# A hybrid decoder step on one core: gate and value rows change banks, token statistics are summed first, and the last convolution adds nothing by DMA

## The chip, the cores and the metric

The kernel runs on one core of a Trainium2 chip. Five engines work side by side, each with its own queue in program order: TensorE (PE in the profile; PEld is its weight load), VectorE (DVE), ScalarE (ACT), GpSimd (POOL) and SyncE (SP). SP starts the ordinary transfers, GpSimd the transfers that add into their destination. The metric is the device time of one execution in microseconds; lower is better.

## The reference

One layer of a decoder for 1024 prompt tokens and 8 sample tokens (1032 columns), width 1024, all in float32. Cut to what matters:

```python
h = rmsnorm(x, norm_g)
a_val, a_gl, a_gate, b_u, b_v, b_gate = split(h @ w_in)       # six groups of 1024 columns
a_in  = a_val * sigmoid(a_gl)
a_conv = depthwise_conv(concat([conv_buf, a_in]), conv_w) + conv_b      # 31 taps
a_out = silu(layernorm(a_conv, a_ln_g, a_ln_b)) * silu(a_gate)
gated = spatial_gate(layernorm(b_v, b_ln_g, b_ln_b), w_s, b_s)          # per head, chunks of 128
b_out = b_u * gated * silu(b_gate)
y = rmsnorm(x + concat([a_out, b_out]) @ w_out, final_g)
```

The last 30 rows of `a_in` (prompt and samples) and rows of `b_v` are outputs too.

## The kernel before, in words

**Layout.** Channels lie on the 128 partitions, tokens along the free axis. `w_in` has 48 column tiles of 128 channels: values 0 to 7, sigmoid gates 8 to 15, gates of a 16 to 23, `b_u` 24 to 31, `b_v` 32 to 39, gates of b 40 to 47.

**Units.** A unit makes two column tiles, its row 0 and its row 1 (`mts`, L124): P (value and sigmoid gate of the convolution), v (two tiles of `b_v`), B (`b_u` and its gate, one head), G (two gates of a). There are 24, in the order of L122. The first two, P0 and P1, are worked on together, first for the first half of the tokens and then for the second; each of the others takes all tokens, as two halves (lanes) of 516 columns.

**Seven products for eight.** The two column tiles, the two halves of the 1024 inputs and the two quarters of a lane's tokens form a 2x2 block product, done in Strassen and Winograd's way with seven products (`PRODS`, L36) in place of eight. VectorE makes the sums of weights (`wsum`) and of inputs (`xform`) for it. Float32 precision comes from splitting each operand in two parts, H (ScalarE's rounded copy) and L (VectorE's remainder): H·H + H·L + L·H.

**Slots.** A unit runs in seven slots, a product each, of 24 matmuls over 258 columns. Products gather in PSUM banks: slot 0 writes bank a, slot 1 bank e; then ScalarE copies a to b and e to a tile `p7`; slot 2 adds into b, which ScalarE copies to c; slot 3 adds into a, slot 4 into b, slot 5 into c, slot 6 into b. So a is full after slot 3 (half of row 0), b after slot 4 (half of row 1, still lacking `p7`), c after slot 5 (the other half of row 1, lacking `p7`), and b after slot 6 (the other half of row 0). The next unit's slot 0 writes bank a again.

**Taking the rows out of the banks.** `evac1` (L283): VectorE adds `p7` to bank b or c into row 1; for all but v ScalarE then applies sigmoid or SiLU in place. `evac0` (L272): for v and G ScalarE takes row 0 out of the bank, after slot 3 (L889) and in the next unit's slot 0 (L866). For P and B VectorE multiplies bank a or b by row 1 (L277), in the middle of slot 6 (L870) and in the next unit's slot 0. `finish` (L567) then starts what follows: the convolution for P, a product with the spatial gate `t2` for B.

**Convolution.** `conv_items` (L315) puts a tile's 31 taps on a list. Tap 0 and 1 are ScalarE's (L323, L325), 21 taps are VectorE's, alternately into `c` and `accb` (L333); for the last GT = 8 taps ScalarE makes a product (`gtap`, L341), with every second VectorE tap, and GpSimd adds these by DMA into two of them (L345). `fin` adds `accb` to `c` on VectorE (L356) and the two products by DMA (L358). `acc_item` then adds `c` to the channel sum `ssum` by DMA and stores it (L311, L312).

**LayerNorm behind it.** `mean` (L372) multiplies `ssum` by ones on TensorE. `cen` loads each tile back, subtracts the mean, ScalarE squares, `qacc` sums the squares (L392, L403). `var`, `ln_bc`, then per tile a normalisation and a gate (L456, L462).

**The planner.** `pump` (L99) runs in the middle and at the end of each slot and takes list items while VectorE's planned time is less than 1 us ahead of TensorE's; the program's own prices count, such as MMT = 0.118 a matmul, 1.2 a tap and 1.15 a full row. TensorE items of the list run from slot 3 on; a bar holds `ln_bc` and what follows until all units are done.

**Token statistics.** For each half of the tokens, `stat_x` (L170) squares four x tiles on ScalarE; 48 matmuls of one column sum them over channels; `rstd_x` (L181) takes the root on GpSimd in three pieces; `bcast_x` (L187) spreads it over partitions; `scale_x` (L196) scales x. The first half's come ahead of all products, the second half's in TensorE's queue ahead of slot 0 of the first unit (L833).

**Output.** `w_out` is applied in three groups of columns, each with 8 tiles from b's rows (half 1) and then 8 from a's (half 0), 24 matmuls each (`mmo`, L635); weights are split in two parts as before (L607, L609). Half 0 of group 0 needs the whole LayerNorm.

Of the kernel before, what the change touches and what calls it, by code (L numbers as in the profile page):

```python
# [15 lines left out]
NP_ = 1024  # L16
# [12 lines left out]
GT = 8  # L29
NU = 51  # L30
MMT = 0.118
# [9 lines left out]
def body(ctx, tc, xT, w_in, w_out, state, stateT, conv_w, vecs, wsT, w00, b_s,  # L41
# [80 lines left out]
    units = [(n[0], int(n[1])) for n in ("P0 P1 v0 v1 P2 v2 v3 P3 G0 B0 P4 B1 B2 P5 B3 P6 B4 B5 P7 B6 B7 G1 G2 G3"  # L122
                                         ).split()]
    mts = {"P": lambda k: (k, 8 + k), "v": lambda j: (32 + 2 * j, 33 + 2 * j), "B": lambda h: (24 + h, 40 + h),  # L124
# [43 lines left out]
    CH = tuple((128 * i, n) for i, n in enumerate((128, 128, 2)))  # L168

    def stat_x(p, q, ps):  # L170
        sq = U([128, 2, 2, PW], f"xsq{p}_{q}")
        A.activation(sq, X[p, q], AF.Square)
        for t in range(2):
            for a in range(2):
                for i, (o, n) in enumerate(CH):
                    c = 3 * a + i
                    T.matmul(ps[:n, 0, c:c + 1], lhsT=sq[:, t, a, o:o + n], rhs=ones_m[:, :1],
                             start=(q == 0 and t == 0 and c == 0), stop=(q == 3 and t == 1),
                             skip_group_check=True)

    def rstd_x(p, ps):  # L181
        for (n, a) in ((128, 0), (128, 1), (2, 2)):
            V.tensor_scalar(out=xrs[:n, p, a:a + 4:3], in0=ps[:n, 0, a:a + 4:3], scalar1=EPS, scalar2=None, op0=ALU.add)
            G.tensor_tensor(out=xrs[:n, p, 6 + a:6 + a + 4:3], in0=xrs[:n, p, a:a + 4:3], in1=nhalf[:n, :2],
                            op=ALU.pow)

    def bcast_x(p, ps):  # L187
        for a in range(2):
            for i, (o, n) in enumerate(CH):
                c = 6 + 3 * a + i  # L190
                T.matmul(ps[:, a, o:o + n], lhsT=xrs[:n, p, c:c + 1].to_broadcast([n, 128]), rhs=ident[:n, :n],
                         start=True, stop=True)
        xr[p] = U([128, 2, PW], f"xr{p}")
        A.activation(xr[p], ps[:, :, :PW], AF.Copy)

# [66 lines left out]
    def rows(lanes, r):  # L262
        for u, p in lanes:
            if (u, r) not in row:
                kind, k = units[u]
                if r == 0 and kind == "P":
                    row[u, r] = (U([128, H + NT], f"apad{k}"), H)
                else:
                    row[u, r] = (U([128, NT], f"row{r}_{u}"), 0)
        return {u: row[u, r] for u, p in lanes}  # L270

    def evac0(lanes, z, lohi):  # L272
        kind = units[lanes[0][0]][0]
        if kind in "PB":
            r1 = rows(lanes, 1)
            for (sl, src, dst), (_, _, g) in zip(spots(lanes, rows(lanes, 0), z, lohi), spots(lanes, r1, z, lohi)):
                V.scalar_tensor_tensor(out=dst, in0=src, scalar=-1.0, in1=g, op0=ALU.mult, op1=ALU.mult)  # L277
            dve(0.66)
            return
        for sl, src, dst in spots(lanes, rows(lanes, 0), z, lohi):  # L280
            A.activation(dst, src, FUNC[kind], scale=-1.0)

    def evac1(lanes, z, p7, lohi):  # L283
        kind = units[lanes[0][0]][0]
        for sl, src, dst in spots(lanes, rows(lanes, 1), z, lohi):
            V.tensor_tensor(out=dst, in0=src, in1=p7[:, sl, :], op=ALU.add)
            if kind != "v":
                A.activation(dst, dst, FUNC[kind])
# [13 lines left out]
    cc = {}  # L302

    def acc_item(k):
        def acc():
            c = cc.pop(k)
            if k == 0:
# [5 lines left out]
        fill.append(("dve", 0.0, acc))  # L313

    def conv_items(k, ap):  # L315
        st = {}

# [19 lines left out]
        def gtap(j):  # L337

            def f():
                p = U([128, NP_], f"prod{k}_{j}")  # L340
                A.activation(p, ap[:, j:j + NP_], AF.Copy, scale=cw[:, k, j:j + 1])  # L341
                if j < CW - GT + 2:
# [4 lines left out]
        for j in range(2, CW - GT):  # L347
            fill.append(("dve", 1.2, tap(j)))
            if j % 2 == 0 and j // 2 <= GT:
                fill.append(("dve", 0.0, gtap(CW - GT + j // 2 - 1)))  # L350
            if j == 8 and k:
                acc_item(k - 1)

        def fin():
            c = st["c"]
            V.tensor_tensor(out=c[:, :NP_], in0=c[:, :NP_], in1=st["b"], op=ALU.add)  # L356
            for e in range(2):
                G.dma_start(c[:, :NP_], st.pop(("g", e)), accum_op=ALU.add)  # L358
# [4 lines left out]
    lnc = {}  # L363

    def ln_items():
# [21 lines left out]
        def cen(k):  # L387
            def f():
                c = lnc[k]
                if k < 6:  # L390
# [176 lines left out]
    def finish(u):  # L567
# [3 lines left out]
        if kind == "P":  # L571
            V.memset(r0[:, :H], 0.0)
# [480 lines left out]
```

## Time and profile before

| | us |
|---|---|
| two timed runs | 984.47 and 985.22, median 984.85 |
| the profiled execution | 987.2 |
| its span on the core | 985.3 |
| TensorE busy | 807.6 (82%) |
| VectorE busy | 650.8 (66%) |
| ScalarE busy | 414.1 (42%) |
| GpSimd busy | 82.4 (8%) |
| mean granted TensorE clock | 0.914 |

A row of stretches gives, after its bounds and length, the busy time (and instructions) of PE, PEld, DVE, ACT and POOL, the granted TensorE clock, the share of the DMA engines and GB/s. A group's row gives the source line, the engine, the operation, output<-inputs, shapes and count, then the busy time and the mean duration in ns, then the idle time of that engine just before these instructions and who ended it. A row of the timeline gives start and duration in us, engine, line, operation, and in brackets the idle time before it and who ended it. One matmul of the statistics counts as two records (two passes); those of the products count as one.

### The profile page before, as it was taken

How to read it: one execution, taken by the hardware profiler on the slowest of the kernel's cores; microseconds unless marked ns; L12 is line 12 of the kernel's file. 1: busy time of each engine (PE TensorE's matmuls, PEld its weight loads, DVE VectorE, ACT ScalarE, POOL GpSimd, SP SyncE). 2: the span in 40 equal slices, each digit the busy share in tenths (PEclk: the TensorE clock that was granted, in tenths of full speed). 3: DMA queues.
4: the chain of work that ended last, by engine and by line, in shares of the span. 5: the costliest groups of instructions: out<-in, count | busy, mean ns of one | idle time of the engine just before them, and what ended most of it. 6: DMA issues, size and time to landing. Idle time of an engine off the chain costs nothing. (4 is left out here: it accounts for less than half of the span.)

```text
span 985.3 us, 14147 instructions
## 1 busy us (share of the span) xinstructions
PE 807.6 (82%) x5712; PEld 785.5 (80%) x5712; DVE 650.8 (66%) x805; ACT 414.1 (42%) x562; POOL 82.4 (8%) x103
## 2 busy tenths in 40 slices
PE   7487779979959888998887987999286539999995
PEld 7387779979959888988887887999275528998995
DVE  0527778878875976886767777779245485654754
ACT  2314344545535365354364365346043253513431
POOL 0110001102011111002011101002100000000000
PEclk9997889989979999998989989999688579999998
DMA  7004025658455657458437547449848982284371
GB/s 264 0 1 154 12 66 128 156 135 193 122 140 139 177 136 175 111 132 172 134 94 172 131 115 170 121 109 224 265 145 298 359 327 87 85 286 164 86 258 45
DMA packets 67081, 149.94 MB, mean 152 GB/s; under 512 B 7400, under 2 KB 28584, under 8 KB 67000
## 3 DMA queue, kind: packets, MB, share of 16 engines
q1 hardware_dynamic: 55496, 107.02, 31.9%
q0 software_dynamic: 11520, 42.01, 21.5%
q8 instruction: 45, 0.74, 0.3%
q14 instruction: 20, 0.16, 0.0%
HBM read 84.11 MB, written 28.07 MB: 114 GB/s over the span
## 5 line engine op out<-in xcount | busy, mean ns | idle before, releaser
L244 PE MATMUL za<-hnB,H 128*128 128x258 f32 x384 | 91.4, 325 | 70.7 <-DVE apad L277 41.4
L641 PE MATMUL po<-mh,wh 128*128 128x384 f32 (+1 forms) x384 | 126.2, 329 | 24.2 <-ACT wh L607 16.9
L244 PEld LDWEIGHTS za<-hnB,H 128*128 128x128 f32 x384 | 71.8, 229 | 73.7 <-ACT vh L534 30.5
L641 PE MATMUL po<-mh,wl 128*128 128x384 f32 (+1 forms) x384 | 124.6, 324 | 0.7 <-DVE wl L609 0.7
L641 PE MATMUL po<-ml,wh 128*128 128x384 f32 (+1 forms) x384 | 124.3, 324 | 0.3 <-DVE ml L632 0.3
L155 DVE TENSOR_TENSOR L<-R,H 128x1024 fp32r<-128x1024 f32 x72 | 87.8, 1220 | 48.7 <-ACT H L154 48.3
L333 DVE SCALAR_TENSOR_TENSOR c<-apad,cw,c 128x1024 f32<-128x1024 f32 x88 | 112.4, 1278 | 9.0 <-ACT c L323 9.0
L333 DVE SCALAR_TENSOR_TENSOR accb<-apad,cw,accb 128x1024 f32<-128x1024 f32 x80 | 102.2, 1277 | 0.0
L641 PEld LDWEIGHTS po<-mh,wh 128*128 128x128 f32 x384 | 73.4, 191 | 28.0 <-ACT wh L607 17.2
L154 ACT ACTIVATE H<-R 128x1024 fp32r<-128x1024 f32 x72 | 74.4, 1048 | 37.2 <-DVE R L142 35.9
L244 PE MATMUL za<-hnB,L 128*128 128x258 f32 x384 | 89.1, 319 | 0.0
L244 PE MATMUL za<-lnB,H 128*128 128x258 f32 x384 | 89.0, 318 | 0.0
L244 PE MATMUL zb<-hT,H 128*128 128x258 f32 x384 | 80.9, 292 | 4.4 <-ACT H L154 3.9
L244 PE MATMUL zb<-hT,L 128*128 128x258 f32 x384 | 78.9, 286 | 0.8 <-DVE L L155 0.7
L244 PE MATMUL zb<-lT,H 128*128 128x258 f32 x384 | 78.6, 287 | 0.7 <-DVE lT L230 0.7
L609 DVE TENSOR_TENSOR wl<-wr,wh 128x1024 fp32r<-128x1024 f32 x48 | 58.5, 1223 | 30.1 <-ACT wh L607 28.6
L641 PEld LDWEIGHTS po<-mh,wl 128*128 128x128 f32 x384 | 73.2, 191 | 2.0 <-DVE wl L609 2.0
L641 PEld LDWEIGHTS po<-ml,wh 128*128 128x128 f32 x384 | 73.4, 191 | 0.6 <-DVE ml L632 0.6
L341 ACT ACTIVATE prod<-apad,cw 128x1024 f32<-128x1024 f32 x64 | 73.1, 1143 | 1.5 <-DMA prod<-prod 0.9
L345 POOL DMA_DIRECT2D prod<-prod x48 | 41.2, 859 | 376.0 <-ACT prod L341 316.2
L244 PEld LDWEIGHTS za<-hnB,L 128*128 128x128 f32 x384 | 71.7, 228 | 0.0
L244 PEld LDWEIGHTS za<-lnB,H 128*128 128x128 f32 x384 | 71.3, 226 | 0.0
(149 smaller groups left out, 1632.1 us busy)
## 6 DMA issues: line engine op xcount, KB each, us to landing
R<-w_in SPq DMA_DIRECT2D x96, 256.0 KB, 3.5
prod<-prod POOLq DMA_DIRECT2D x48, 512.0 KB, 5.0
wr<-w_out SPq DMA_DIRECT2D x48, 512.0 KB, 4.6
c<-prod POOLq DMA_DIRECT2D x16, 512.0 KB, 4.6
x<-xT SPq DMA_DIRECT2D x8, 516.0 KB, 8.0
ssum<-c POOLq DMA_DIRECT2D x8, 516.0 KB, 7.0
cD<-c POOLq DMA_DIRECT2D x8, 516.0 KB, 8.2
sgD<-row SPq DMA_DIRECT2D x8, 516.0 KB, 4.8
```

The lines of the kernel that those rows point to most:

```text
L154: A.activation(h, r, AF.Copy)
L155: V.tensor_tensor(out=l, in0=r, in1=h, op=ALU.subtract)
L244: T.matmul(z[:, s, :PW], lhsT=HL[u, wi][we][:, wh, cs], rhs=F[name, p][xe][:, kt, :], start=first, stop=(kt == 3 and we == 1), skip_group_ ...
L333: V.scalar_tensor_tensor(out=o, in0=ap[:, j:j + NP_], scalar=cw[:, k, j:j + 1], in1=o, op0=ALU.mult, op1=ALU.add)
L341: A.activation(p, ap[:, j:j + NP_], AF.Copy, scale=cw[:, k, j:j + 1])
L345: G.dma_start(st["g", j % 2], p, accum_op=ALU.add)
L609: V.tensor_tensor(out=wl[s], in0=r, in1=wh[s], op=ALU.subtract)
L641: T.matmul(z, lhsT=w[:, cs], rhs=m_[g, half, kt][e], start=(half == 1 and kt == 0 and e == 0 and w is wh[s]), stop=(half == 0 and kt == KT ...
```

## The change

- P and B swap their rows: row 0 is now the gate, row 1 the value. ScalarE applies sigmoid or SiLU with a sign change straight from bank a after slot 3 and from bank b in the next unit's slot 0, as for v and G; VectorE's sums with `p7` give the value; in `finish` one multiplication over 1032 columns joins them, on VectorE. Only G keeps an in-place SiLU on row 1.
- Ten taps go to ScalarE and the adding DMAs for tiles 0 to 6, one with each of VectorE's first ten taps, and none for tile 7, whose 29 other taps are VectorE's. Tile 7 is added to the channel sum by VectorE and stays on the chip.
- P7 moves ahead of B5, MMT becomes 0.12.
- x is loaded ahead of the weights. The squares of four x tiles are summed on VectorE, then 12 matmuls of one column (six token groups of 86, two halves) sum over channels; the root is taken in one piece. 16 and 24 matmuls without a use (`warm`) stand before the first half's statistics and behind its broadcast. The second half's statistics go into the slots of the first unit: squares after slot 1, sums after slot 2, matmuls after slot 3, broadcast after slot 4.

```diff
-GT = 8
+GTS = (10,) * 7 + (0,)
-MMT = 0.118
+MMT = 0.12
...
-    units = [... "P0 P1 v0 v1 P2 v2 v3 P3 G0 B0 P4 B1 B2 P5 B3 P6 B4 B5 P7 B6 B7 G1 G2 G3" ...]
-    mts = {"P": lambda k: (k, 8 + k), ..., "B": lambda h: (24 + h, 40 + h),
+    units = [... "P0 P1 v0 v1 P2 v2 v3 P3 G0 B0 P4 B1 B2 P5 B3 P6 B4 P7 B5 B6 B7 G1 G2 G3" ...]
+    mts = {"P": lambda k: (8 + k, k), ..., "B": lambda h: (40 + h, 24 + h),
...
+    CN = PW // 3
+    def square_x(p, q):
         sq = U([128, 2, 2, PW], f"xsq{p}_{q}")
         A.activation(sq, X[p, q], AF.Square)
+        xsq[p, q] = sq
+    def sum_x(p):
+        for q in range(1, 4):
+            V.tensor_tensor(out=xsq[p, 0], in0=xsq[p, 0], in1=xsq.pop((p, q)), op=ALU.add)
+        dve(3.5)
+    def stat_x(p, ps):
+        sq = xsq.pop((p, 0))
+        for c in range(6):
+            for t in range(2):
+                T.matmul(ps[:CN, 0, c:c + 1], lhsT=sq[:, t, c // 3, CN * (c % 3):CN * (c % 3) + CN], rhs=ones_m[:, :1],
+                         start=t == 0, stop=t == 1)
     def rstd_x(p, ps):
+        V.tensor_scalar(out=xrs[:CN, p, :6], in0=ps[:CN, 0, :6], scalar1=EPS, scalar2=None, op0=ALU.add)
+        G.tensor_tensor(out=xrs[:CN, p, 6:], in0=xrs[:CN, p, :6], in1=nhalf[:CN, :6], op=ALU.pow)
...
+    def warm(n):
+        p = PS("e", f"warm{slotno[0]}_{n}")
+        for _ in range(n):
+            T.matmul(p[:, 0, :128], lhsT=ones_m, rhs=ident, start=True, stop=True)
...
     def evac0(lanes, z, lohi):
-        kind = units[lanes[0][0]][0]
-        if kind in "PB":
-            r1 = rows(lanes, 1)
-            for (sl, src, dst), (_, _, g) in zip(spots(lanes, rows(lanes, 0), z, lohi), spots(lanes, r1, z, lohi)):
-                V.scalar_tensor_tensor(out=dst, in0=src, scalar=-1.0, in1=g, op0=ALU.mult, op1=ALU.mult)
-            dve(0.66)
-            return
         for sl, src, dst in spots(lanes, rows(lanes, 0), z, lohi):
-            A.activation(dst, src, FUNC[kind], scale=-1.0)
+            A.activation(dst, src, FUNC[units[lanes[0][0]][0]], scale=-1.0)
     def evac1(lanes, z, p7, lohi):
...
-            if kind != "v":
-                A.activation(dst, dst, FUNC[kind])
+            if units[lanes[0][0]][0] == "G":
+                A.activation(dst, dst, AF.Silu)
...
         def acc():
             c = cc.pop(k)
+            if k == 7:
+                V.tensor_tensor(out=Ssum[0], in0=Ssum[0], in1=c, op=ALU.add)
+                lnc[7] = c
+                return
...
-        for j in range(2, CW - GT):
+        for j in range(2, CW - gt):
             fill.append(("dve", 1.2, tap(j)))
-            if j % 2 == 0 and j // 2 <= GT:
-                fill.append(("dve", 0.0, gtap(CW - GT + j // 2 - 1)))
-            if j == 8 and k:
+            if j < 2 + gt:
+                fill.append(("dve", 0.0, gtap(CW - gt + j - 2)))
+            if j == 10 and k:
                 acc_item(k - 1)
...
-            for e in range(2):
-                G.dma_start(c[:, :NP_], st.pop(("g", e)), accum_op=ALU.add)
+            if gt:
+                for e in range(2):
+                    G.dma_start(c[:, :NP_], st.pop(("g", e)), accum_op=ALU.add)
...
         if kind == "P":
-            V.memset(r0[:, :H], 0.0)
+            V.memset(r1[:, :H], 0.0)
+            V.tensor_tensor(out=r1[:, H:], in0=r1[:, H:], in1=r0, op=ALU.mult)
+            dve(1.25)
...
         if kind == "B":
-            V.tensor_tensor(out=r0, in0=r0, in1=t2.pop(k), op=ALU.mult)
-            dve(1.15)
+            V.tensor_tensor(out=r1, in0=r1, in1=t2.pop(k), op=ALU.mult)
+            V.tensor_tensor(out=r1, in0=r1, in1=r0, op=ALU.mult)
+            dve(2.3)
...
-                if slot == 6 and kind in "PB":
-                    evac0(lanes, Z.pop("a"), 0)
...
-                elif slot == 3 and kind not in "PB":
+                elif slot == 3:
                     evac0(lanes, Z.pop("a"), 0)
```

The start, with the places where the second half's statistics go:

```diff
+        for q in range(4):
+            load_x(0, q)
         for u in range(2):
             wload(u, 1)
...
-        for q in range(4):
-            stat_x(0, q, p)
+        for q in range(4):
+            square_x(0, q)
+        sum_x(0)
+        warm(16)
+        p = PS("e", "xst0")
+        stat_x(0, p)
         rstd_x(0, p)
         for u in range(2):
             wsum(u, "S3")
+            wsum(u, "S1")
             wsplit(u, 1)
-            wsum(u, "S1")
         bcast_x(0, PS("e", "xbc0"))
-        p1 = PS("a", "xst1")
+        warm(24)
...
                 if slot == 1:
                     xform(0, "nB21")
+                    for q in range(4):
+                        square_x(1, q)
                 if slot == 2:
...
+                    sum_x(1)
                 if slot == 3:
...
+                    p = PS("e", "xst1")
+                    stat_x(1, p)
+                    rstd_x(1, p)
                 if slot == 4:
+                    bcast_x(1, PS("e", "xbc1"))
```

More of the change, by code (lines that the diff above doesn't have):

```diff
@@ L119, in slot_end @@
             outq.popleft()[1]()
-    units = [(n[0], int(n[1])) for n in ("P0 P1 v0 v1 P2 v2 v3 P3 G0 B0 P4 B1 B2 P5 B3 P6 B4 B5 P7 B6 B7 G1 G2 G3"
+    units = [(n[0], int(n[1])) for n in ("P0 P1 v0 v1 P2 v2 v3 P3 G0 B0 P4 B1 B2 P5 B3 P6 B4 P7 B5 B6 B7 G1 G2 G3"
                                          ).split()]
-    mts = {"P": lambda k: (k, 8 + k), "v": lambda j: (32 + 2 * j, 33 + 2 * j), "B": lambda h: (24 + h, 40 + h),
+    mts = {"P": lambda k: (8 + k, k), "v": lambda j: (32 + 2 * j, 33 + 2 * j), "B": lambda h: (40 + h, 24 + h),
            "G": lambda q: (16 + 2 * q, 17 + 2 * q)}
@@ L166, in load_x @@
                      xT[256 * q:256 * q + 256, 2 * PW * p:2 * PW * (p + 1)].rearrange("(t p) s -> p t s", p=128))
-    CH = tuple((128 * i, n) for i, n in enumerate((128, 128, 2)))
-    def stat_x(p, q, ps):
+    CN = PW // 3
+    xsq = {}
+    def square_x(p, q):
         sq = U([128, 2, 2, PW], f"xsq{p}_{q}")
         A.activation(sq, X[p, q], AF.Square)
[L173 to L179, printed above, removed]
+        xsq[p, q] = sq
@@ L181, in rstd_x @@
+    def sum_x(p):
[8 more added lines that the diff above has]
+                         start=t == 0, stop=t == 1)
     def rstd_x(p, ps):
[L182 to L185, printed above, removed]
+        V.tensor_scalar(out=xrs[:CN, p, :6], in0=ps[:CN, 0, :6], scalar1=EPS, scalar2=None, op0=ALU.add)
+        G.tensor_tensor(out=xrs[:CN, p, 6:], in0=xrs[:CN, p, :6], in1=nhalf[:CN, :6], op=ALU.pow)
@@ L187, in bcast_x @@
     def bcast_x(p, ps):
[L188 to L192, printed above, removed]
+        for c in range(6):
+            T.matmul(ps[:, c // 3, CN * (c % 3):CN * (c % 3) + CN], lhsT=xrs[:CN, p, 6 + c:7 + c].to_broadcast([CN, 128]),
+                     rhs=ident[:CN, :CN], start=True, stop=True)
@@ L265, in rows @@
                 kind, k = units[u]
-                if r == 0 and kind == "P":
+                if r == 1 and kind == "P":
                     row[u, r] = (U([128, H + NT], f"apad{k}"), H)
@@ L302, in body @@
     cc = {}
+    lnc = {}
     def acc_item(k):
@@ L312, in acc @@
             G.dma_start(cD[k], c)
-        fill.append(("dve", 0.0, acc))
+        fill.append(("dve", 1.15 if k == 7 else 0.0, acc))
     def conv_items(k, ap):
         st = {}
+        gt = GTS[k]
         def start():
@@ L341, in f @@
                 A.activation(p, ap[:, j:j + NP_], AF.Copy, scale=cw[:, k, j:j + 1])
-                if j < CW - GT + 2:
+                if j < CW - gt + 2:
                     st["g", j % 2] = p
@@ L389, in f @@
                 c = lnc[k]
-                if k < 6:
+                if k < 5:
                     lnload(k + 2)
@@ L742, in body @@
     with tc.manual_schedule():
+        for q in range(4):
+            load_x(0, q)
         for u in range(2):
             wload(u, 1)
-        for q in range(2):
-            load_x(0, q)
         SP.dma_start(vec, vecs)
-        for q in range(2, 4):
-            load_x(0, q)
-        for u in range(2):
-            wload(u, 4)
-        for u in range(2):
-            wload(u, 3)
+        for i in (4, 3, 2):
+            for u in range(2):
+                wload(u, i)
         for q in range(4):
             load_x(1, q)
-        for u in range(2):
-            wload(u, 2)
         SP.dma_start(cw, conv_w)
@@ L832, in body @@
                 if slot in (0, 1):
-                    if si == 0 and slot == 0:
-                        for q in range(4):
-                            stat_x(1, q, p1)
-                        rstd_x(1, p1)
                     Z[bank] = PS(bank, f"z{bank}{si}")
```

10 lines of the change are left out of this document (3 added, 7 removed).

## The prediction, made before the changed kernel ran

> **What bounds the kernel now.** I read the span in stretches first, then the groups by line with what ended the idle time before them, then the timeline around the longest waits.
>
> ```profile
> span 985.3 us, 14147 instructions
> core 0: us, PE busy (x) PEld busy (x) DVE busy (x) ACT busy (x) POOL busy (x), PEclk, DMA share, GB/s
> 60.98:135.80 74.82, 54.06 (x348) 50.82 (x349) 51.81 (x75) 28.79 (x42) 4.33 (x4) 0.87 0.20 65
> 135.80:696.44 560.64, 497.81 (x3856) 491.59 (x3856) 434.33 (x515) 272.55 (x374) 64.99 (x78) 0.93 0.59 145
> 662.88:683.32 20.44, 20.44 (x171) 20.23 (x169) 19.32 (x21) 12.28 (x17) 5.51 (x7) 1.00 0.90 221
> 584.21:614.65 30.44, 25.41 (x186) 25.07 (x187) 21.22 (x25) 16.11 (x24) 4.88 (x6) 0.89 0.65 152
> 728.90:810.24 81.34, 44.36 (x230) 42.22 (x228) 49.90 (x51) 32.82 (x38) 2.19 (x2) 0.76 0.85 318
> 810.24:985.30 175.06, 158.56 (x1002) 154.25 (x1002) 94.93 (x136) 60.33 (x87) 3.28 (x4) 0.97 0.42 142
> ```
>
> The stretches are: the first two units; v0 to the fifth slot of G3; unit G2 alone; unit B6 alone; the first output tiles, up to the second half of group 0; the rest. G2 shows a unit that nothing stops: 20.44 us of unbroken TensorE, with VectorE already busy 19.32. B6 took 30.44: TensorE was busy 25.41 and idle 5.03. A gate adds 2.02 in the planner's price (L553, L562), so some 3 us of the busy time is slow clock (0.89). TensorE sets the pace of this stage; what can be won is its idle time and what that does to its clock. Who ends the idle time:
>
> ```profile
> L244 PE MATMUL za<-hnB,H 128*128 128x258 f32 x384 | 91.4, 325 | 70.7 <-DVE apad L277 41.4 <-DVE row L277 28.8 <-DVE xrs L183 0.5
> L155 DVE TENSOR_TENSOR L<-R,H 128x1024 fp32r<-128x1024 f32 x72 | 87.8, 1220 | 48.7 <-ACT H L154 48.3
> L341 ACT ACTIVATE prod<-apad,cw 128x1024 f32<-128x1024 f32 x64 | 73.1, 1143 | 1.5 <-DMA prod<-prod 0.9 <-DVE L L155 0.6
> prod<-prod POOLq DMA_DIRECT2D x48, 512.0 KB, 5.0
> ```
>
> 70.2 us of TensorE's idle time end with L277, VectorE's multiplication out of bank a, which the next unit's first product needs. (The last row, of the page's list of transfers, is used below.)
>
> **Start (term A).**
>
> ```profile
> 8.90 17.08 PE L177 MATMUL xst<-ones_m,xsq 128*128 128x1 f32 x96 [3.56 <-ACT xsq L172]
> 11.97 1.06 ACT L172 ACTIVATE xsq<-x 128x1032 f32<-128x1032 f32 x1 [0.29 <-DMA x<-xT]
> 33.32 2.75 DVE L198 SCALAR_TENSOR_TENSOR x<-x,vec,xr 128x516 f32<-128x516 f32 x4
> 35.99 1.48 DVE L214 SCALAR_TENSOR_TENSOR lnB<-x,hnB 128x516 fp32r<-128x516 f32 x2
> 42.48 1.23 DVE L230 TENSOR_TENSOR lnT<-tnT,hnT 128x1032 fp32r<-128x1032 f32 x1 [1.13 <-ACT hnT L229]
> 43.45 17.07 PE L177 MATMUL xst<-ones_m,xsq 128*128 128x1 f32 x96 [11.35 <-ACT xsq L172]
> 60.80 1.81 POOL L184 TENSOR_TENSOR xrs<-xrs,nhalf 128x2 f32<-128x2 f32 x1 [31.00 <-DVE xrs L183]
> 60.98 0.77 PE L244 MATMUL za<-hnB,H 128*128 128x258 f32 x2 [0.47 <-DVE xrs L183]
> 104.74 0.77 PE L244 MATMUL za<-hnB,H 128*128 128x258 f32 x2 [5.26 <-DVE apad L277]
> 135.80 0.55 PE L244 MATMUL za<-hnB,H 128*128 128x258 f32 x1 [5.76 <-DVE apad L277]
> ```
>
> Twice TensorE spends 17.1 us on 96 records (48 matmuls of one column, two passes each, 0.178 us a record), and the second lot stands ahead of the first product although lnB was ready at 37.5. After the change each lot has 24 records, 4.3 us. First half: x loads before two weights of 256 KB, so the last square ends some 1.5 earlier than 13.0, at 11.5; the third add ends at 12.7 (1.23 each by the lnT row, two of them between the squares); statistics 17.0, or less if the 16 warm matmuls, which fit into TensorE's idle time, raise the clock; I take 16. From 26.0 (8.90 + 17.08) to the first scaling, at 33.3, took 7.3 us, mostly weight sums on VectorE, now with one wait less: 6.4, so the scaling starts at 22.4 and lnB, 4.1 behind it as before, ends at 26.5. The weights now queue behind x, but their sums come only after 16. The first product starts at 26.5 for 60.98: -34.5. The 24 warm matmuls lie in the wait before it.
>
> The second half's statistics move into unit 0: four squares (4.2 us) on ScalarE ahead of its bank copies, three adds (3.7) on VectorE ahead of nT4, 24 records in TensorE's queue ahead of slot 4, then GpSimd's pow (1.8) and the broadcast ahead of slot 5. VectorE is the tight engine of the first two units (51.81 of 74.82). All hidden it costs 0, all in series about 15; I follow the queues (ScalarE's squares delay the copy to c by about 3, the adds 3.7, pow and broadcast 3.3) and take 10. Both L277 stalls go, 5.26 + 5.76 = 11.0. v0 then starts at 135.8 - 34.5 + 10 - 11.0, about 100: **A = -36** (-28 to -46).
>
> **The units (term B).** How the stall before B6 came about, beside G2:
>
> ```profile
> 579.08 0.64 ACT L288 ACTIVATE row<-row 128x516 f32<-128x516 f32 x1 [1.21 <-DVE row L286]
> 579.62 1.64 ACT L534 ACTIVATE vh<-vh,rs 128x128 f32<-128x128 f32 x4
> 582.24 1.22 DVE L155 TENSOR_TENSOR L<-R,H 128x1024 fp32r<-128x1024 f32 x1 [2.00 <-ACT H L154]
> 583.38 0.69 DVE L277 SCALAR_TENSOR_TENSOR apad<-za,row 128x516 f32<-128x516 f32 x1
> 584.21 0.77 PE L244 MATMUL za<-hnB,H 128*128 128x258 f32 x2 [3.02 <-DVE apad L277]
> 584.78 0.63 PE L244 MATMUL za<-lnB,H 128*128 128x258 f32 x2
> 663.12 0.40 PE L244 MATMUL za<-lnB,H 128*128 128x258 f32 x2
> 674.62 0.60 ACT L281 ACTIVATE row<-za 128x516 f32<-128x516 f32 x1 [2.22 <-PE za L244]
> core 0: us, ACT busy (x), PEclk, DMA share, GB/s
> 662.88:683.32 20.44, 5.71 (x5) 1.00 0.90 221
> ```
>
> Bank a is full after slot 3 but held until ScalarE has made the gate of the other bank (579.08), then its v_norm and a split, and VectorE has finished a remainder and multiplied (583.38). After the 3.02 us a pair of matmuls takes 0.63 instead of 0.40. With the change P and B give bank a to ScalarE after slot 3, as G2 does at 674.62, three slots before it is needed. The work is nearly unchanged: ScalarE has two gate calls a unit either way; VectorE trades two multiplications of 516 columns (0.69 each) for one of 1032 (1.23).
>
> 21.64 units at G2's 20.44 are 442.3; eight gates add 16.2, the four v units 7.9 (L480, L488), L728 1.7: 468 of the 560.6 us. So 92.5 is stall and slow clock: the whole prize. What comes back: ten taps instead of eight go to ScalarE, with every tap instead of every second. G2 has five of them in its 12.28 us of ScalarE (the last row, of L341 alone: 5.71); with ten (1.143 each) and the two opening calls of a conv (L323, L325, alike in size) such a unit needs 20.4 of 20.4. ScalarE also waits in order for the ends of slots 0 to 3, 2.22 us at 674.62; I take 5 a unit. So up to 5 us in each of seven convs, 0 to 36; nearest is G2 with nothing, but at half the rate, so I take the middle, 18, with its clock. GpSimd issues 56 adding transfers for 48; in a unit where a conv opens one falls due every 2.4 us (half of VectorE's time goes to the list), and two chains at 5.0 us to landing just carry that; where they lag, products hold buffers that SP's weight loads wait for. VectorE's one product for P and B now waits at slot 0 for ScalarE's gate of bank b; taps and the split HL stand behind it, but a sum and an L (1.9 us) ahead of it, so it costs nothing unless ScalarE is late. I put 2 on both: **B = -72** (-92 to -40). VectorE's own list shrinks by six taps (162 for 168).
>
> The stalls kept cost clock as well. By the rows, 3.02 us of idle time slowed B6 by some 3 us. By the Trainium skill (TensorE: Matmul & The Clock Gate, Part 1) the clock halves after an idle window of about 3.4 us, so stalls shorter than that would be free of it. Seven stalls of 1.8 would then cost 13, a sum of 820; if each slows as B6's did, 34, a sum of 841; my 20 lies between.
>
> **The last conv (terms C and D).**
>
> ```profile
> 649.36 1.22 DVE L356 TENSOR_TENSOR c<-c,accb 128x1024 f32<-128x1024 f32 x1
> 695.10 1.22 DVE L356 TENSOR_TENSOR c<-c,accb 128x1024 f32<-128x1024 f32 x1
> 696.96 0.85 POOL L358 DMA_DIRECT2D c<-prod  x1 [10.12 <-DVE c L356]
> 716.62 3.64 PE L376 MATMUL lnm<-ssum,ones_m 128*128 128x512 f32 x4 [20.18 <-DMA ssum<-c]
> 722.01 1.23 DVE L392 TENSOR_TENSOR lc<-lc,lnmean 128x1032 f32<-128x1032 f32 x1 [25.69 <-ACT lnmean L380]
> 770.33 3.70 PE L415 MATMUL lnv<-ones_m,lnq 128*128 128x1 f32 x18 [16.00 <-DVE lnq L403]
> 781.95 2.38 DVE L456 TENSOR_TENSOR ma<-ma,lnr 128x1032 f32<-128x1032 f32 x2 [7.66 <-ACT lnr L441]
> 810.24 0.69 PE L641 MATMUL po<-mh,wh 128*128 128x384 f32 x1 [16.92 <-ACT wh L607]
> ```
>
> The mean (L376) stands in TensorE's queue inside G3 and waits for three transfers, one after another: 20.18 us, and with its own matmuls and copies 25 until 722. Now the last sum is one VectorE add (1.2) and the mean follows it. Left are VectorE's lag, the 3.64 and a copy: 6. **C = -19** (-10 to -23).
>
> The planner also gets there sooner. Its list (1.2 a tap, 1.3 around them) shrinks from 8 x 26.5 to 7 x 24.1 + 37.3 with the add, by 6; MMT 0.12 grants 0.34 a unit, 7 over 22 units; the gates free 2; less 2 lost in rounding: 13. A G unit leaves 12 us for the list, so the mean comes 1.1 units earlier, within G2, and the 16 sums behind it (L392, L403, 18.4 planned) are just done at G3's end instead of lasting from 722 to 770. That P7 comes a unit earlier adds nothing: conv 6 ended at 649.4 while P7's products had ended before 584.2, so the list never ran dry. What remains from the first output matmul to the second half: 2.6 until the statistics, 11.6 from 770.33 to 781.95, 28.3 from there to 810.24, and six weight splits, 1.22 each as L155's, that now fall among them: 50 for 81.3. **D = -31** (-45 if half of it hides under the tiles, -5 if the sums are late). From there on nothing changes: 175.
>
> **Sum:** -36 - 72 - 19 - 31 = -158. The profiled execution spans 985.3 (987.2 in all, 2.35 above the median of 984.85); taken from the median: 827.
>
> **The rivals.**
> - *ScalarE's queue takes bank a's place* (for it: 20.4 of 20.4 in the units where a conv opens, and VectorE already waits 48.3 us for ScalarE's H; against: G2). B keeps 56 to 60 us of stall and slow clock instead of 20: about 865. The Trainium skill (TensorE: Matmul & The Clock Gate, Architectural detail) has ScalarE's queue strictly in order; the trace agrees, with the split's H behind four v_norms at 579.62.
> - *The sums do not fit into G2 and G3* (for it: 18.4 planned into 18, with VectorE at 95%; against: loads of c are issued two ahead). D is lost: 858.
> - *The change does little because the split L, not L277, is what is late* (582.24 waits 2.00 for ScalarE): half of the 59 us of idle time left to B stays (30), with the clock that it costs (15): 872. Against: L sits ahead of L277 in VectorE's queue, and L277 is what TensorE names 16 times.
> - *Other side: TensorE stays at half clock.* Were each unit cut by a wait like B6's and the clock never back, a unit would take 20.44 x 0.63 / 0.40 = 32. It decides above 1004, that is 177 us more than forecast at 11.8 a unit: 15 of 22 units. Only B6's 3 us speak for it; G2 keeps 1.00 with the same queues.
>
> **How the numbers follow.** Forecast 0.60 (800 to 850), first rival 0.17, second 0.12, third 0.08, other side 0.03. The range runs from 793 (B and D at their best ends, 20 and 14 below) to 880 (the first rival with A or C at its worst end, 8 or 9; the third with A's). About 2% is what a measurement of this kernel can tell from no change; the rivals but the last are far below 965, so faster 0.96, same 0.02, slower 0.02.
>
> **What would show it.** A: first product near 27, v0 near 100, two xst groups of 24. B: no releaser L277; P and B units of 21 to 24 us; idle time before za below 15. C: no wait for ssum. D: lnv right after the first po matmuls. It is wrong if waits for ScalarE (bank copies, H) grow to over 40 us before zb or VectorE's L, or if lnq still ends tens of us into the output stage.

## The result, and the profile after

The changed kernel takes 877.53 us (median of 2 runs, 876.83 to 878.22) against 984.85: a ratio of 0.891 with an interval of 0.887 to 0.895. That is 107 us less, where 158 less was forecast. It is faster, and inside the range (793 to 880) by 2.5 us only. The profiled execution spans 875.0 us, 110.3 less than the one before; the table of terms below goes by these two executions.

The same stretches as before, cut at the same events (columns: stretch, length, busy time and instructions of PE, PEld, DVE, ACT, POOL, granted clock, DMA share, GB/s). The third row is unit P3 alone; the second row is to be held against the row of the kernel before that stands under them:

```profile
core 0: us, PE busy (x) PEld busy (x) DVE busy (x) ACT busy (x) POOL busy (x), PEclk, DMA share, GB/s
27.82:97.73 69.91, 52.84 (x376) 50.43 (x375) 49.52 (x69) 33.02 (x45) 2.39 (x2) 0.85 0.20 65
97.73:639.20 541.47, 493.98 (x3925) 485.61 (x3923) 450.44 (x520) 292.29 (x397) 71.96 (x86) 0.96 0.70 177
218.93:254.18 35.25, 27.90 (x188) 26.78 (x187) 23.48 (x35) 17.06 (x22) 7.84 (x10) 0.81 0.76 169
639.20:700.27 61.07, 42.64 (x230) 41.11 (x228) 35.41 (x39) 25.30 (x31) 2.19 (x2) 0.81 0.86 324
700.27:875.00 174.73, 158.12 (x1002) 153.80 (x1002) 94.96 (x136) 60.35 (x87) 3.28 (x4) 0.97 0.41 143
```
```profile
135.80:728.90 593.10, 508.98 (x3923) 500.29 (x3923) 439.52 (x521) 277.76 (x381) 68.09 (x82) 0.92 0.59 148
```

The first product starts at 27.82 and v0 at 97.73, both within 3 us of the forecast. From v0 to the first output matmul (639.20) the kernel takes 541.5; before it was 593.1 (135.80 to 728.90). The rest to the second half takes 61.1 for 81.3, and the end is the same as before (174.7 for 175.1). P3 is a unit that still stalls: TensorE is busy 27.90 of 35.25 at a clock of 0.81, with ScalarE busy only 17.06.

| term | forecast | measured | from |
|---|---|---|---|
| A, start | -36 | -38.1 | v0 at 97.73 for 135.80 |
| B, units | -72 | -29.8 | 593.1 to 541.5, less C |
| C, mean | -19 | -21.8 | TensorE held 3.4 for 25.2 |
| D, behind the units | -31 | -20.3 | 61.07 for 81.34 |
| the rest | 0 | -0.3 | 174.73 for 175.06 |

The terms add up to -110 instead of -158, so 48 us are missing; B alone fell short by 42, D by 11, and A and C each won some 2 or 3 more than forecast. Who ends the idle time now, by group (busy time, mean ns of one, idle time before, and who ended it), and below them the row of GpSimd's adds in the kernel before, and the row of the page's list of transfers for the adds of the changed one:

```profile
L252 PE MATMUL za<-hnB,H 128*128 128x258 f32 x384 | 77.4, 283 | 0.0
L252 PE MATMUL zb<-hT,H 128*128 128x258 f32 x384 | 85.8, 307 | 29.3 <-ACT zb L885 21.4 <-ACT H L154 4.4 <-ACT zc L893 3.5
L252 PE MATMUL zb<-hnB,HL 128*128 128x258 f32 x384 | 70.7, 299 | 15.1 <-DVE apad L286 11.9 <-DVE row L286 3.0
L155 DVE TENSOR_TENSOR L<-R,H 128x1024 fp32r<-128x1024 f32 x72 | 87.8, 1220 | 72.0 <-ACT H L154 39.1 <-DMA prod<-prod 13.9 <-ACT p L889 7.5
L347 ACT ACTIVATE prod<-apad,cw 128x1024 f32<-128x1024 f32 x70 | 78.3, 1144 | 29.9 <-DMA prod<-prod 18.6 <-DMA c<-prod 9.8 <-DVE apad L578 1.1
L351 POOL DMA_DIRECT2D prod<-prod x56 | 48.4, 864 | 208.3 <-ACT prod L347 109.7 <-DMA prod<-prod 67.9 <-issue 14.0
```
```profile
L345 POOL DMA_DIRECT2D prod<-prod x48 | 41.2, 859 | 376.0 <-ACT prod L341 316.2 <-issue 22.1 <-DMA prod<-prod 17.6
```
```profile
prod<-prod POOLq DMA_DIRECT2D x56, 512.0 KB, 6.0
```

The stall that was to go is gone: nothing stands before za, where 70.7 us stood. New idle time stands before zb: 21.4 us for ScalarE's copy of bank a into b (L885) and 11.9 for VectorE's sum that reads row 1 out of bank b (L286), before slot 6 may add into it. Further back, ScalarE's products wait 28.4 us for transfers that add (18.6 + 9.8; 0.9 before), and GpSimd itself waits 67.9 us for its own earlier adds (17.6 before). These land in 6.0 us (median) instead of 5.0.

How that reaches TensorE shows the timeline of P3 (start, duration, engine, line, operation, in brackets the idle time and who ended it):

```profile
225.60 0.84 POOL L365 DMA_DIRECT2D c<-prod  x1 [7.09 <-DMA c<-prod]
231.40 1.15 ACT L347 ACTIVATE prod<-apad,cw 128x1024 f32<-128x1024 f32 x1 [6.84 <-DMA c<-prod]
232.45 0.58 ACT L889 ACTIVATE p<-ze 128x516 f32<-128x516 f32 x1
233.09 1.42 PE L483 MATMUL vp<-ident,row 128*128 128x128 f32 x8 [2.45 <-ACT p L889]
...
232.93 2.18 ACT L347 ACTIVATE prod<-apad,cw 128x1024 f32<-128x1024 f32 x2
...
235.53 2.17 ACT L347 ACTIVATE prod<-apad,cw 128x1024 f32<-128x1024 f32 x2
235.54 0.84 POOL L351 DMA_DIRECT2D prod<-prod  x1 [9.09 <-ACT prod L347]
...
240.69 0.85 POOL L351 DMA_DIRECT2D prod<-prod  x1 [2.76 <-DMA prod<-prod]
243.51 0.84 POOL L351 DMA_DIRECT2D prod<-prod  x1 [1.97 <-DMA prod<-prod]
245.77 1.23 DVE L155 TENSOR_TENSOR L<-R,H 128x1024 fp32r<-128x1024 f32 x1 [11.77 <-DMA prod<-prod]
```

GpSimd has two sums of a finished conv to join to `c`; the second waits 7.09 us for the first to land. ScalarE's product at 231.40 needs a buffer and waits 6.84 us for these transfers to land; the copy `p` of bank e stands behind it, and TensorE's next work waits 2.45 us for that. Then five products come within 6.3 us (231.40 to 237.70), GpSimd waits for earlier adds to land and issues one every 2.8 us (240.69, 243.51), and VectorE stands 11.77 us before a remainder L, until an add has landed and with it a buffer is free.

### The profile page after: what moved, and what is told of

It is laid out like the page before. It is cut to its first block, busy times and chain, and to the rows that moved or that the text cites. A ratio compares the mean times of both kernels' runs of the same rounds, so it can differ in the third digit from the quotient of the medians.

```text
span 875.0 us, 13987 instructions
## 1 busy us (share of the span) xinstructions
PE 768.8 (88%) x5648; PEld 751.0 (86%) x5648; DVE 646.6 (74%) x782; ACT 420.5 (48%) x568; POOL 82.4 (9%) x103
## 5 line engine op out<-in xcount | busy, mean ns | idle before, releaser
L155 DVE TENSOR_TENSOR L<-R,H 128x1024 fp32r<-128x1024 f32 x72 | 87.8, 1220 | 72.0 <-ACT H L154 39.1
L252 PE MATMUL zb<-hT,H 128*128 128x258 f32 x384 | 85.8, 307 | 29.3 <-ACT zb L885 21.4
L339 DVE SCALAR_TENSOR_TENSOR c<-apad,cw,c 128x1024 f32<-128x1024 f32 x85 | 108.6, 1278 | 2.4 <-ACT c L329 2.4
L347 ACT ACTIVATE prod<-apad,cw 128x1024 f32<-128x1024 f32 x70 | 78.3, 1144 | 29.9 <-DMA prod<-prod 18.6
L252 PEld LDWEIGHTS zb<-hT,H 128*128 128x128 f32 x384 | 64.6, 206 | 32.1 <-ACT zb L885 22.7
L252 PE MATMUL zb<-hnB,HL 128*128 128x258 f32 x384 | 70.7, 299 | 15.1 <-DVE apad L286 11.9
L252 PE MATMUL za<-lnB,H 128*128 128x258 f32 x384 | 77.3, 283 | 0.4 <-DVE lnB L222 0.4
L252 PE MATMUL za<-hnB,H 128*128 128x258 f32 x384 | 77.4, 283 | 0.0
L252 PE MATMUL za<-hnB,L 128*128 128x258 f32 x384 | 77.4, 283 | 0.0
L252 PEld LDWEIGHTS zb<-hnB,HL 128*128 128x128 f32 x384 | 58.3, 203 | 17.2 <-DVE apad L286 13.0
L351 POOL DMA_DIRECT2D prod<-prod x56 | 48.4, 864 | 208.3 <-ACT prod L347 109.7
```

The source lines that it names most:

```text
L155: V.tensor_tensor(out=l, in0=r, in1=h, op=ALU.subtract)
L252: T.matmul(z[:, s, :PW], lhsT=HL[u, wi][we][:, wh, cs], rhs=F[name, p][xe][:, kt, :], start=first, stop=(kt == 3 and we == 1), skip_group_ ...
L339: V.scalar_tensor_tensor(out=o, in0=ap[:, j:j + NP_], scalar=cw[:, k, j:j + 1], in1=o, op0=ALU.mult, op1=ALU.add)
L351: G.dma_start(st["g", j % 2], p, accum_op=ALU.add)
```

## The experiments

Three theories stood against each other for the 42 us that B fell short by. The first (the first rival): ScalarE's own load of ten products and the bank copies. The second: products wait to be added and hold buffers that loads, products and splits need. The third: GpSimd's queue of adds, two chains in which each add waits for the one before, is too slow for products at one per tap; two kernels try two forms of it (3a), the pace of the products and the number of chains, against the mere amount of adding traffic (3b). Unless a count is given, a kernel was run once; five runs of one and the same kernel (`z1_pace` and `w3_pace`) lay between 841.4 and 849.3, so a difference of less than 8 us between single runs is not read.

**The parts alone.** `y1_evac` is the kernel before with the swap of rows alone, `y2_stats` the one before with the new start alone.

> The kernel before with the swap of rows and banks alone (gates by ScalarE from banks a and b, value rows by VectorE's sums, one product in finish); start, convolution and planner as before. All theories: no TensorE wait ends with L277. If the pace of the products (one with each tap) is what cost term B, this kernel, with one product for every second tap, should win nearly the whole prize: the 11 us of the first two units and 75 to 90 of 92, so 885 to 900. If the swap itself makes ScalarE late (its gate calls now wait for slots 0 and 3), it wins 11 and some 30: 935 to 950.

> The kernel before with the start alone (x loaded first, squares summed on VectorE, 24 records a half, warm matmuls, second half's statistics inside the first unit). Term A without the 11 us of waits that belong to the swap: -24 to -30, so 955 to 961; if the start was gained only because the banks were free earlier, above 965.

`y1_evac` took 892.2 and `y2_stats` 959.2, beside 984.2 for the kernel before. The swap alone gives 92, of which 9 lie in the first two units (65.7 for 74.8) and belong to term A; the other 83 are still more than the 72 of term B. The start gives 25. The two parts give 117, and the whole change 107: something in the third part costs. The windows of `y1_evac` from v0 to the first output matmul, and on to the second half:

```profile
126.53:614.06 487.53, 476.04 (x3918) 471.71 (x3916) 439.55 (x511) 277.32 (x381) 65.97 (x79) 0.99 0.69 172
614.06:714.62 100.56, 48.44 (x237) 43.75 (x235) 52.63 (x53) 35.04 (x41) 4.45 (x5) 0.74 0.84 298
```

With the old convolution the units run at a clock of 0.99 and TensorE is idle for 11.5 of 487.5 us. Nearly all of the prize was there.

**Everything but the third part.** `y3_oldconv` undoes in the changed kernel the ten taps, their pace, the last tile's path, the order of P7 and MMT:

```diff
-GTS = (10,) * 7 + (0,)
+GTS = (8,) * 8
-MMT = 0.12
+MMT = 0.118
...
-            if k == 7:
-                V.tensor_tensor(out=Ssum[0], in0=Ssum[0], in1=c, op=ALU.add)
...
-            if j < 2 + gt:
-                fill.append(("dve", 0.0, gtap(CW - gt + j - 2)))
+            if j % 2 == 0 and j // 2 <= gt:
+                fill.append(("dve", 0.0, gtap(CW - gt + j // 2 - 1)))
```

> The changed kernel with the third part undone: convolution list, last tile, order of P7 and B5 and MMT as before (eight taps by ScalarE, one with every second of VectorE's, adding transfers for the last tile too); swap of banks and new start stay. The swap alone gave 892.2 and the start alone 959.2 for 984.2. If the parts are independent: 892.2 - 25.1 = 867, some 10 us less than with the third part, which then costs more by its adding transfers than it gains behind the last tile. If the third part gains what terms C and D showed (about 40 us) and costs nothing: 900 to 920.

It took 862.1, beside 986.8 for the kernel before: 125 less than that, and 15 less than the changed kernel. Its windows (units; then first output matmul to second half):

```profile
99.58:584.23 484.65, 475.57 (x3918) 471.36 (x3917) 440.64 (x511) 277.22 (x381) 65.85 (x79) 0.99 0.69 173
584.23:685.40 101.17, 48.24 (x236) 43.61 (x234) 51.68 (x53) 35.03 (x41) 4.44 (x5) 0.74 0.83 297
```

So the third part wins 40.1 behind the units (101.17 to 61.07), as C and D had it together, and costs 56.8 inside them (484.65 to 541.47). Of these 18.4 are busy TensorE time for practically the same matmuls (475.57 to 493.98, clock 0.99 to 0.96); the other 38.4 are idle. A part of both figures is the same work in another place: in `y3_oldconv` the mean runs behind the units (604.78) and the 16 sums after it, in the changed kernel the mean runs inside them (602.01), and most of the sums.

**The adds taken away.** `x1_noadd` makes all products but leaves out the 56 adds; `x3_free` adds a slice of the padded input instead, so that each product is free at once and the number of adds stays.

```diff
                 if j < CW - gt + 2:
                     st["g", j % 2] = p
-                else:
-                    G.dma_start(st["g", j % 2], p, accum_op=ALU.add)
```
```diff
-                    G.dma_start(st["g", j % 2], p, accum_op=ALU.add)
+                    G.dma_start(st["g", j % 2], ap[:, j:j + NP_], accum_op=ALU.add)
```

> The changed kernel, but the products of taps 23 to 30 are made by ScalarE and not added (the adding transfers of L351 are left out, so eight of the ten taps of each tile are missing from the result). Theory 1 (ScalarE's load: ten products plus the rest fill a unit): ScalarE does the same work, so the time stays within 10 us of 877.5. Theory 2 (buffers: the adding transfers, in two chains, land too slowly, products hold their buffers, ScalarE waits in order for one, and the bank copies behind it come late): the waits of ScalarE and VectorE for prod transfers (18.6 + 16.5 + 13.9 us) and most of TensorE's 21.4 us of waits for the copy to b go; 835 to 850.

> The changed kernel, but each adding transfer of L351 reads a slice of the padded input instead of ScalarE's product (the result is wrong by the weights of those taps). ScalarE makes all products, as many transfers run over the same two chains, but a product's buffer is free as soon as it is written. Theory 1 (ScalarE's load): 868 to 885. Theory 2 (buffers held by the adds): 835 to 850, close to the kernel without adds. Theory 3 (the adding traffic itself slows other transfers and GpSimd's queue, whoever holds buffers): 868 to 885 here, and 835 to 850 only without adds.

`x1_noadd` took 839.7: 38 less. Its units, and the group that waited longest for ScalarE:

```profile
97.63:602.29 504.66, 483.41 (x3924) 476.31 (x3923) 450.47 (x521) 290.47 (x397) 24.11 (x30) 0.98 0.44 132
```
```profile
L252 PE MATMUL zb<-hT,H 128*128 128x258 f32 x384 | 83.1, 299 | 16.4 <-ACT zb L883 7.2 <-ACT H L154 4.9 <-ACT zc L891 4.2
```

ScalarE does the same (290.47 us, 397 instructions, for 292.29 and 397), yet the units take 36.8 less and the waits for the copy into bank b fall from 21.4 to 7.2. For these 37 us the first theory falls: ScalarE's load is the same, at the same pace, and the adds are the cost. `x3_free` took 873.8, which single runs do not tell from the changed kernel. What was saved on products was lost elsewhere; in its views of waits (engine, line, releaser: total us, times, longest) stand

```profile
POOL prod L351 <- DMA prod<-apad: 128.8, 41, 7.7
SPq L135 <- DMA cD<-c: 58.7, 3, 24.8
```

GpSimd waited longer for its own adds than in the changed kernel (128.8 for 67.9), and the loads of weights (SP's queue) waited for a store of `c`, which stands in GpSimd's queue behind the adds; ScalarE's H waited 26.6 us for such stores too. So, by this run, the buffers of the products alone are not the cause either: the queue of adds holds whatever stands behind it.

**Pace, count and chains.** The next kernels keep the tenth product and the last tile's path, and change only how products reach the chains: one with every second tap (`z1_pace`), the same with eight (`z2_pace8`, seven tiles), or four chains joined in pairs at the old pace (`z3_chains4`).

```diff
-            if j < 2 + gt:
-                fill.append(("dve", 0.0, gtap(CW - gt + j - 2)))
+            if j % 2 == 0 and j // 2 <= gt:
+                fill.append(("dve", 0.0, gtap(CW - gt + j // 2 - 1)))
```
```diff
-                if j < CW - gt + 2:
-                    st["g", j % 2] = p
+                if j < CW - gt + 4:
+                    st["g", (j - CW + gt) % 4] = p
...
                 for e in range(2):
+                    G.dma_start(st["g", e], st.pop(("g", e + 2)), accum_op=ALU.add)
+                for e in range(2):
                     G.dma_start(c[:, :NP_], st.pop(("g", e)), accum_op=ALU.add)
```

> The changed kernel, ten products a tile, but one with every second tap of VectorE instead of with each. Theory 3a (GpSimd's queue: two chains of adds cannot take a product with each tap, and the stores, sums and buffers behind them come late): at half the rate each chain has some 10 us for an add that lands in 6, the waits go: 838 to 852. Theory 3b (the amount of adding traffic slows all transfers): as many adds, 865 to 880.

> As z1, with eight products for tiles 0 to 6 (none for tile 7). 42 adds into products instead of 56, and 14 taps (17 us planned) more on VectorE's list, so the mean comes about 1.4 units later, in the last unit, and some of the LayerNorm's sums fall behind the units. Theory 3a: stalls as in z1, end later by 15 to 30 us: 855 to 875. Theory 3b: fewer transfers pay: below z1.

> The changed kernel with a product for each tap, but the products go into four chains instead of two, joined in pairs at the end. As many adding transfers, and a chain gets an add only with every fourth tap. Theory 3a (waits for the landing of the chain before): most of GpSimd's 68 us of waits for its own adds go, 840 to 858. Theory 3b (amount of traffic): 868 to 885.

`z1_pace`, the same ten products and 56 adds at half the pace, took 849.3, 28 less. Its units, and GpSimd's adds in it:

```profile
99.53:611.71 512.18, 486.37 (x3925) 479.33 (x3923) 450.86 (x521) 292.03 (x397) 71.95 (x86) 0.98 0.74 188
L351 POOL DMA_DIRECT2D prod<-prod x56 | 48.4, 872 | 296.2 <-ACT prod L347 248.3 <-DMA prod<-prod 28.7 <-ACT row L282 5.8
```

The units take 512.2 for 541.5, and GpSimd waits 28.7 us for its own adds instead of 67.9. As many adds, landing in the same 6.0 us, cost 28 less: the amount of traffic (3b) is not what these 28 us are. `z2_pace8` took 854.5: its units are shorter still (497.6), but VectorE's longer list ends later and the second half starts 81.1 after the first output matmul; 3a had 855 to 875 for it. `z3_chains4` went the other way, 887.0, more than 3a or 3b had given it. The adds into its chains wait only 7.0 us for one another, but the adds that join the chains wait 43.3, and all land in 7.3 us instead of 6.0; and it has four products per tile to keep until the end instead of two. SP's loads waited twice as long for adds. The same row of SP's own waits in the changed kernel, then in `z3_chains4`:

```profile
SPq L135 <- DMA prod<-prod: 59.2, 7, 14.7
```
```profile
SPq L135 <- DMA prod<-prod: 117.3, 11, 35.7
```

Two things changed at once here, so this run does not part the waits along a chain from the buffers that four chains hold. Nor are SP's waits the price: in `z1_pace`, 28 us faster than the changed kernel, this row is 66.5.

**Fewer buffers.** All working tiles share NU = 51 buffers; `w1_nu49` gives the changed kernel 49, `w2_pace49` gives 49 to the one with the slower pace.

```diff
-NU = 51
+NU = 49
```

> The changed kernel with 49 of the 51 row buffers (NU), nothing else. If buffers are what the late adds take away, two fewer make ScalarE, VectorE and the weight loads wait more: 890 to 930. If the adds cost by their traffic or by GpSimd's queue alone, buffers do not matter: within 6 us of 877.5.

> The kernel of z1 (ten products, one with every second tap; 849.3) with 49 of 51 row buffers. If buffers are the currency, a part of what the slower pace won is lost again: 860 to 880. If the pace works by traffic alone: within 6 us of 849.

`w1_nu49` took 904.2, 27 more than with 51, and `w2_pace49` 881.4, 32 above 849.3 (36 above the median of `w3_pace`), just above what was expected if buffers count. In `w1_nu49` SP's loads and ScalarE's products wait for adds still longer (59.2 and 18.6 us with 51 buffers):

```profile
SPq L135 <- DMA prod<-prod: 99.0, 11, 18.3
```
```profile
L347 ACT ACTIVATE prod<-apad,cw 128x1024 f32<-128x1024 f32 x70 | 78.7, 1144 | 60.1 <-DMA prod<-prod 46.2 <-DMA c<-prod 7.6 <-PE zc L252 3.4
```

So the number of buffers bears on the time in both kernels, also where the pace is slow. That late adds keep them from being freed is read from the waits. Over the whole execution, the waits of ScalarE and VectorE for transfers that add (into a product or into `c`), those of SP's queue for the same, and the length of the units (v0 to the first output matmul), for the kernels that compute the whole and keep the last tile's path, in us:

| kernel | units | ScalarE and VectorE wait for adds | SP waits for adds |
|---|---|---|---|
| `z2_pace8` | 497.6 | 22.6 | 52.8 |
| `w4_pace9` (next) | 498.7 | 22.6 | 67.8 |
| `w3_pace` (next) | 511.7 | 43.6 | 115.9 |
| `z1_pace` | 512.2 | 50.6 | 116.6 |
| the changed kernel | 541.5 | 68.5 | 79.0 |
| `w2_pace49` | 545.4 | 77.3 | 142.0 |
| `z3_chains4` | 550.2 | 86.1 | 137.3 |
| `w1_nu49` | 566.0 | 100.4 | 132.8 |

The units follow the waits of ScalarE and VectorE, and not those of SP. It is an order, not a proof, and the two kernels that leave something out do not fall into it: `x1_noadd` has 11.6 and units of 504.7, and `x3_free` 8.1 and 536.0, where the two engines wait another 31.7 us for stores of `c` behind the adds.

**A better version.** `w3_pace` is `z1_pace` run four times, and `w4_pace9` has nine products per tile at the slower pace (GTS = (9,) * 7 + (0,)), run four times too.

> The kernel of z1 again, timed in rounds: 849, that is a ratio of 0.862 to the kernel before and 0.968 to the changed one. If z1's single look was an outlier, above 860.

> As w3 with nine products for tiles 0 to 6: 49 adds into products for 56, seven taps (8 us planned) more on VectorE's list. Units shorter by some 7 us (between 512 in z1 and 498 in z2), the end of the sums later by about as much: 847 to 855, within 4 us of w3.

`w3_pace` took 845.4 (ratio 0.856 to the kernel before, 0.853 to 0.859), `w4_pace9` 838.8 (0.850, 0.846 to 0.853), more below it than was expected: no run of the one reaches into those of the other (841.4 to 846.0, 837.8 to 839.8). It is the fastest of all that compute the whole. Its units, its way to the second half and two groups:

```profile
99.91:598.59 498.68, 480.45 (x3925) 474.46 (x3924) 453.94 (x524) 283.29 (x388) 65.93 (x79) 0.99 0.72 183
598.59:662.50 63.91, 43.48 (x230) 42.12 (x229) 39.71 (x42) 27.58 (x33) 2.19 (x2) 0.79 0.84 322
```
```profile
L252 PE MATMUL zb<-hT,H 128*128 128x258 f32 x384 | 82.6, 297 | 14.0 <-ACT zb L885 7.8 <-ACT H L154 4.9 <-ACT zc L893 1.2
L351 POOL DMA_DIRECT2D prod<-prod x49 | 42.7, 872 | 279.3 <-ACT prod L347 223.4 <-DMA prod<-prod 23.9 <-DVE c L339 11.6
```

GpSimd now waits for ScalarE's products (223.4 for 109.7) and little for its own adds (23.9 for 67.9): the adds keep up. The wait before zb is down to 14.0 from 29.3, the clock is back at 0.99, and the second half still starts 64 us after the first output matmul. The third part is worth about 23 us in this form (862.1, one run, to 838.8) instead of costing 15.

**Left open.** How much of the 37 us goes through buffers that late adds hold, and how much through what stands behind them in GpSimd's queue, was not separated. Nor why the units of `x1_noadd` take 20 more than those of `y3_oldconv` (504.7 for 484.7) without any adds of products: it has the mean (563.62) and the LayerNorm sums inside its units, where `y3_oldconv` has them behind, but these were not tried alone, and ScalarE's ten products are an equal candidate. More than 51 buffers were not tried.

## Why the prediction was right and wrong

**Direction and the waits that were to go: right.** Each of the three named in it went: the one before za, that of the mean, and the two lots of 96 records of statistics. The likeliest time was 50 us too low. That 877.5 still lies in the range is luck: its upper end, 880, came from the third rival, whose cause did not show.

**A (-36, measured -38.1): right, by parts that offset each other.** The first product was forecast at 26.5 and came at 27.82. Its input was ready earlier than forecast, at 24.25, but the 24 warm matmuls (48 records) did not lie in the wait before it: they ended at 28.06, and the first product stood behind them in TensorE's queue.

```profile
19.68 8.38 PE L202 MATMUL warm<-ident,ones_m 128*128 128x128 f32 x48 [0.69 <-ACT xr L197]
22.77 1.48 DVE L222 SCALAR_TENSOR_TENSOR lnB<-x,hnB 128x516 fp32r<-128x516 f32 x2
```

That probably cost less than the 3.6 us it looks like, since TensorE then waited 2.02 and 2.37 us for ScalarE's H at 35.81 and 38.76; fewer warm matmuls were not tried. The second half's statistics were to give back 10 of the 11 us of the two L277 stalls; the first two units shrank by 4.9, so they gave back 6. The statistics stood 6.31 us in TensorE's queue behind VectorE's sums, as the queues had it:

```profile
52.90 3.65 PE L185 MATMUL xst<-ones_m,xsq 128*86 128x1 f32 x24 [6.31 <-DVE xsq L178]
```

**B (-72, measured -30): the step that failed.** The prize of 92.5 was read rightly in the main: with the old convolution the units take 484.7, against 567.9 before without the mean's hold, which is 83 less. What failed is the 2 us put on GpSimd's adds and on VectorE's one product together. The step held two numbers against each other, a product due every 2.4 us and two chains that land in 5.0, and found that these "just carry that". With no margin, an add that lands in 6.0 already lags (two chains then take one per 3.0), and the list does not hand out its items evenly: in P3 five products came within 6.3 us and were added one every 2.8. The same sentence named the consequence, buffers that SP's loads wait for, but not that ScalarE's next product and H and VectorE's L take theirs from the same store and stand in order ahead of the bank copies and sums; it is these waits, not SP's, that go with the time. The runs put 37 us on the adds (`x1_noadd`), 28 on their pace alone (`z1_pace`). The 18 us allowed for ScalarE's load were not tried alone; the 20 that the units of `x1_noadd` still lose may be these or the work that moved inside.

**The rivals.** The third (L, not L277) gave the nearest time, 872, by luck: it fell with `y1_evac`, where the swap left 11.5 us of idle time. The first (ScalarE's queue) gave 865 and was right about where TensorE would wait, for another reason: in the 37 us that went with the adds, ScalarE was late because it waited, not because it was full. The sign named for it, waits for ScalarE that grow to over 40 us, could not decide: 29.3 us before zb, and before L 39.1 for H with 7.5 for the copy `p`, where 48.3 had stood before the change. The second (sums too late) came true in part, under D. Of the other side nothing showed: the clock over the units rose from 0.92 to 0.96.

**The clock.** The stalls that stayed cost clock again. Two waits of the changed kernel, each with the pair of matmuls behind it:

```profile
152.33 0.50 PE L252 MATMUL zb<-hT,H 128*128 128x258 f32 x2 [2.19 <-ACT zb L885]
152.67 0.40 PE L252 MATMUL zb<-lT,H 128*128 128x258 f32 x2
...
264.26 0.68 PE L252 MATMUL zb<-hT,H 128*128 128x258 f32 x2 [4.18 <-ACT zb L885]
264.73 0.63 PE L252 MATMUL zb<-lT,H 128*128 128x258 f32 x2
```

After 2.19 us a pair still takes 0.40, after 4.18 it takes 0.63. By the Trainium skill (TensorE: Matmul & The Clock Gate, Part 1) an idle window of about 3.4 us, free-running, halves the clock. These two rows agree. Others do not: the 3.02 us before B6 in the kernel before were followed by pairs of 0.63, and so, a few matmuls later, were 2.04 us at 499.41 in the changed kernel, while 2.36 us at 630.46 were not. So a stall shorter than 3.4 us is not free of it, as one bound of the prediction had it. Of the 18.4 us of extra busy time in the units about 2 are the mean's own matmuls; the rest goes with the clock, 0.96 for 0.99.

**C (-19, measured -22): right.** No wait for `ssum` is left, and the mean runs inside G2, as the planner's sum had it. **D (-31, measured -20): right in kind, too large.** The tail of the LayerNorm in the changed kernel:

```profile
602.01 1.88 PE L382 MATMUL lnm<-ssum,ones_m 128*128 128x512 f32 x4
605.63 2.38 DVE L398 TENSOR_TENSOR lc<-lc,lnmean 128x1032 f32<-128x1032 f32 x2 [5.29 <-ACT lnmean L386]
645.84 1.23 DVE L409 TENSOR_TENSOR lnq<-lnq,lns 128x1032 f32<-128x1032 f32 x1
647.23 1.97 PE L421 MATMUL lnv<-ones_m,lnq 128*128 128x1 f32 x18
649.93 1.06 ACT L616 ACTIVATE wh<-wr 128x1024 fp32r<-128x1024 f32 x1 [5.27 <-DMA wr<-w_out]
652.16 0.16 DVE L423 TENSOR_SCALAR rs<-lnv 128x8 f32<-128x8 f32 x1
660.02 1.23 DVE L462 TENSOR_TENSOR ma<-ma,lnr 128x1032 f32<-128x1032 f32 x1 [7.64 <-ACT lnr L447]
700.27 0.69 PE L650 MATMUL po<-mh,wh 128*128 128x384 f32 x1 [11.65 <-ACT wh L616]
```

The 16 sums were to end with G3; the last began 6.6 us after the first output matmul (645.84 for 639.20), so the statistics came after 8.0 instead of 2.6. From there to the first normalisation it was 12.8 for 11.6: the small step on the root (L423) stood in VectorE's queue behind a weight split that waited for ScalarE's `wh`, itself 5.27 us late by a load. From the normalisation to the second half it was 40.3 for 35.6. Together 11 us, that is the 50 that became 61.

## What to carry to other kernels

When work is handed to transfers that add, compare the pace of its products with the time that the slowest chain needs, and ask for a margin: equal rates here (one per 2.4 us against one per 2.5) left no room for a landing in 6.0 us, and each product in the queue holds a buffer that other engines need. Spreading the same products over twice the time won 28 us here, and leaving out the tenth product at that pace some 7 more. And try the parts of a change each alone: two parts together were worth more than all three.

## What the runs showed that was not expected

- Four independent chains were not faster than two but, in one run, some 9 us slower (887.0 for 877.5). The likely reason, not tried alone, is that each keeps a base product alive: the waits of ScalarE and VectorE for adds went from 68.5 to 86.1 us.
- Two of 51 buffers are worth 27 us in the changed kernel, and 32 to 36 in the one with the slower pace, although fewer waits for adds are left there (50.6 us for 68.5).
- Left with nothing to add, TensorE's units kept a clock of 0.98; the same units with 56 adds had 0.96 and 10.6 us more busy time (493.98 for 483.41). Waits of a few us in other engines came back as slow clock on the one that bounds.
